# Three pairs of k tiles instead of two in two products, and a multiplication moved to ScalarE

## The chip, the cores and the metric

The kernel runs on one core of a Trainium2 chip. The metric is the time of one execution on the device in microseconds (us). Three runs of the kernel before took 1409.82, 1412.84 and 1413.8 us; the median is 1412.84 us.

## The reference

One block of a streaming encoder on 256 tokens of width 2048, in float32. Cut to what matters here:

```python
z = rms_norm(x, norm_mix_w) @ w_in                    # 2048 -> 11264
# an HGRN2 recurrence gives y_a, chunked attention gives y_b
merged = gate_a * (y_a @ w_branch_a) + gate_b * (y_b @ w_branch_b)
h = x + merged @ w_out                                # 2048 -> 2048
u = rms_norm(h, norm_mlp_w)
h = h + square(relu(u @ w_up)) @ w_down               # 2048 -> 8192 -> 2048
out = rms_norm(h, norm_final_w)
```

The change lies between `merged @ w_out` and `u @ w_up`.

## The kernel before, in words

**Precision.** Every float32 operand is split into a high part of a rounded type (fp32r) and a low part, the rest. A product of two tiles is three matmuls, high by high, high by low and low by high (`mm3`, L143 to L145). The split (`split`, L88) is a cast on ScalarE (L89) and a subtraction on VectorE (L90). Weights come from HBM in pieces of 128 x 1024 (two k tiles of 512 columns), are split in the same way, and lie in eight raw and six high and six low buffers.

**The GEMM unit.** Most of the gates, w_out, w_up and w_down go through `gemm_s` (L718). A unit makes 256 tokens by 1024 output columns, as a 2 x 2 arrangement of accumulators: two blocks of 128 tokens (`m`) by two blocks of 512 columns (`n`). The 16 k tiles of 128 would give 16 x 4 = 64 products. For some k tiles it uses the scheme of Strassen and Winograd: k tile k is paired with k tile k + 4, and each pair takes seven products (named p1 to p7) in place of eight, at the price of additions of weight pieces on VectorE (`add`, L742) and of sums of activation blocks that are made once (`combos`, `S2`, `S4`, `S5`, `S7`, which have three pairs each). The parameter `r` says how many pairs go through the scheme. With `r=2` the weights of the scheme are four whole pieces (`W11`, `W12`, `W21`, `W22`). With `r=3` the third pair's weights come in two more pieces, `X` and `Y`, that each hold two halves from different places, with additions of 512 columns, three more whole splits (`px`, `py`, `px2`) and a half one (`p4y`). The k tiles left over are plain products (`plain`): with `r=2` six pairs of k tiles for each `n`, with `r=3` five, the first of which is k tiles 3 and 7.

**The order in a unit.** p1, p3, p5, p2; then `flush()` does what the unit before left for later (its last plain product and the end of its second column block); then p6, a plain product, p7. If the second remaining pair of k tiles needs only activation blocks that exist (`early`, L843), another plain product comes next, then p4. Otherwise half of a plain product stands ahead of p4 and half behind it. Then `between()` is called, which turns activations for what follows; the remaining plain products end the unit. In the `early` order the first plain products behind `between()` are on the first two pairs of k tiles in the list of those left over; in the other order on the second alone, which is k tiles 8 and 9 with `r=3`.

**The three units around the change.** `wo0` and `wo2` are the two units of w_out, `up00` and `up02` the first two of w_up. At `between()` of `wo2` stands `h_blocks(0)`, at that of `up00` `h_blocks(2)` (L932). For two blocks n and two token blocks m each, it transposes h with four PE transposes into one PSUM bank (two banks are there for this), multiplies by the norm's weight, which is one factor per partition for each group of 128 columns, into `tmp` (`hw`, L941), splits that into the high and low part of `hT` (ScalarE and VectorE), and sums the squares of h on ScalarE (`hsq`, L943). `h_blocks(0)` then makes the sums S from `hT`. At the start of `up00` two of the four blocks of `hT` exist; the first w_down unit `dn00` starts in the same way with two blocks of its own activations.

**What sets the order of the work.** A planner orders the instructions of each engine by priority, mostly program order, with its own estimate of when inputs and buffers are ready; work marked with high priority (weight splits, additions of pieces, evictions) goes ahead on its engine. Each engine then takes its instructions in that order. All weights are loaded through SP's queue; ScalarE and POOL issue a few other transfers.

Of the kernel before, what the change touches and what calls it, by code (L numbers as in the profile page):

```python
# [11 lines left out]
AF = mybir.ActivationFunctionType  # L12
ALU = mybir.AluOpType
# [3 lines left out]
P = 128  # L17
# [4 lines left out]
FF = 8192  # L22
NC = 512
# [13 lines left out]
def bc(ap, pos, n):  # L37

    dims = [list(d) for d in ap.ap]
    dims.insert(pos, [0, n])  # L40
    return bass.AP(tensor=ap.tensor, offset=ap.offset, ap=dims)
# [9 lines left out]
def tile_hybrid_block(  # L51
# [5 lines left out]
    nc = tc.nc  # L57
# [13 lines left out]
    wmix, wmlp = vt[:, 0:16], vt[:, 16:32]  # L71
# [16 lines left out]
    def split(hi, lo, src, copy=None):  # L88
        (copy or nc.scalar.copy)(hi, src)  # L89
        nc.vector.tensor_tensor(lo, src, hi.bitcast(F32), op=ALU.subtract)  # L90
# [7 lines left out]
    def new_act(what):  # L98

        return apool.tile([P, 4, 2, T], F32R, name=f"act_{what}", tag="act")  # L100

    def transpose4(src, what):

        tp = turns_in.tile([P, 4, P], F32, name=f"tp_{what}", tag="tp")
        for j in range(4):
            nc.tensor.transpose(tp[:, j, :], src[:, j * P:(j + 1) * P], ident)
        return tp
# [42 lines left out]
    def gemm(lhs, w, n0, nkt, what, wide=False, between=None):  # L150

        acc = new_acc(what)
        for kt, wh, wl in weights(w, n0, nkt, NC, what, wide=wide):
            if between and between[0][0] == kt:
                between.pop(0)[1]()
            for m in range(NM):
                mm3(acc[:, m, :], *lhs_of(lhs, kt, m), wh, wl, kt == 0, kt == nkt - 1)
        return acc
# [48 lines left out]
    done = [0, 0]  # L207
    for kt, n in zip(starts, steps):
        c, a = kt // 4, kt % 4
# [376 lines left out]
    for g in range(2):  # L586
        qT = [qk_chunk(C_AQ + g * NC + i * T, f"aq{g}{i}", rstd8_t, None if g or i else acc_q0) for i in range(2)]
        kT = [qk_chunk(C_AK + g * NC + i * T, f"ak{g}{i}", rstd_t) for i in range(2)]
        acc = gemm(xT, w_in_n, C_AV + g * NC, KD, f"av{g}")
# [14 lines left out]
    def token(what):  # L604
        return tk.tile([P, NC], F32, name=what, tag="t", bufs=TOK)
# [7 lines left out]
    R = 3  # L613
# [36 lines left out]
    for n in range(2):  # L650
        acc = gemm(xT, w_in_t, C_GA + n * NC, KD, f"ga{n}", wide=True)
# [52 lines left out]
    def gemm2(lhs, w, n0, nkt, what):  # L704

        acc = [bank(f"{what}{m}") for m in range(NM)]
        for k in range(0, nkt, 2):
            wh, wl = parts(piece(w, f"{what}{k}", (n0, k), (n0, k + 1)), f"{what}{k}")
            for m in range(NM):
                for a in range(2):  # L710
                    mm3(acc[m], *lhs_of(lhs, k + a, m), wh[:, a], wl[:, a], k + a == 0, k + a == nkt - 1)
        return acc

    def evict(dst, acc):
        with tc.high_priority(offset=2000):
            nc.vector.tensor_tensor(dst, acc, dst, op=ALU.add)
# [178 lines left out]
    for gates, c, col, what, fresh in ((ga, 2, C_GA, "ga", True), (gb, 0, C_GB, "gb", True), (gb, 2, C_GB, "gb", False)):  # L895
        gates += [[None] * NM for _ in range(2)]

        def done(m, n, acc, gates=gates, c=c, what=what):
            gates[c + n][m] = sigmoid(token(f"gate_{what}{c + n}{m}"), acc, m)
# [5 lines left out]
    mT = []  # L905
# [8 lines left out]
    for n in range(4):  # L914
        for y, w, gate, what in ((ya, w_branch_a, ga[n], "ba"), (yb, w_branch_b, gb[n], "bb")):
            acc = gemm2(y, w, n * NC, 8, f"{what}{n}")
            for m in range(NM):
                nc.vector.tensor_tensor(gate[m], acc[m], gate[m], op=ALU.mult)
            if what == "ba" and n:
                turn(n - 1)  # L920
                if n == 2:
                    Sm = combos(mT, "m", "b")
# [4 lines left out]
    h1 = [[None] * NM for _ in range(4)]  # L927
    ssq2 = small.tile([P, NM, 4], F32, name="ssq2", tag="ssq2")
    hT = []
    Sh = {}  # L930

    def h_blocks(n0):  # L932

        for n in (n0, n0 + 1):
            hT.append(new_act(f"h{n}"))
            hi, lo = hT[n][:, :, 0, :], hT[n][:, :, 1, :]
            for m in range(NM):
                t = h1[n][m]
                tp = transpose4(t, f"h{n}{m}")
                tmp = tk.tile([P, 4, P], F32, name=f"hw_{n}_{m}", tag="t", bufs=TOK)  # L940
                nc.vector.tensor_tensor(tmp, tp, bc(wmlp[:, 4 * n:4 * n + 4], 2, P), op=ALU.mult)  # L941
                split(hi[:, :, m * P:(m + 1) * P], lo[:, :, m * P:(m + 1) * P], tmp)
                nc.scalar.activation(token(f"hsq_{n}_{m}"), t, AF.Square, accum_out=ssq2[:, m, n:n + 1])  # L943
        if not n0:
            Sh.update(combos(hT, "h", "a"))
            return
        ssum2 = small.tile([P, NM], F32, name="ssum2", tag="ssum")
        nc.vector.tensor_reduce(ssum2, ssq2, axis=AX.X, op=ALU.add)
        rsqrt(rstd2, ssum2, D, NM)

    rstd2 = const.tile([P, NM], F32, name="rstd2")
    for n0 in (0, 2):
        for n in (n0, n0 + 1):
            for m in range(NM):
                t = token(f"h1_{n}_{m}")
                nc.gpsimd.dma_start(t, x[m * P:(m + 1) * P, n * NC:(n + 1) * NC])
                h1[n][m] = t
        gemm_s(mT, Sm, w_out, n0 * NC, f"wo{n0}", lambda m, n, acc, n0=n0: evict(h1[n0 + n][m], acc), r=2 if n0 else R,
               between=lambda: h_blocks(0) if n0 else turn(3))


# [3 lines left out]
    NQ = 4  # L965
    for qd in range(NQ):
        last = qd == NQ - 1
        uT = []
        pend = []

        def turn():

            c, rs = pend.pop(0)
            uT.append(new_act(f"u{qd}{c}"))
            hi, lo = uT[-1][:, :, 0, :], uT[-1][:, :, 1, :]
            for m in range(NM):
                tp = transpose4(rs[m], f"u{qd}{c}{m}")
                if c < 2:
                    blocks[m, c] = tk.tile([P, pairs, P], F32, name=f"a{m}{c}_u{qd}", tag="t", bufs=TOK)
                    nc.scalar.copy(blocks[m, c], tp[:, :pairs])  # L980
                split(hi[:, :, m * P:(m + 1) * P], lo[:, :, m * P:(m + 1) * P], tp)

        Su = {}
        blocks = {}
        pairs = R if last else 4

        def turns():
            if len(hT) == 2:
                h_blocks(2)
            while pend:  # L990
                turn()
            if len(uT) == 2:
                Su.update(combos(uT, f"u{qd}", "b", [blocks[m, j] for m in range(NM) for j in range(2)], pairs))

        for c in range(0, 4, 2):
            rs = {}

            def done(m, n, acc, c=c, rs=rs):
                t = token(f"r{qd}{c}")
                with tc.high_priority(offset=2000):  # L1000
                    nc.scalar.activation(t, acc, AF.Relu, scale=rstd2[:, m:m + 1])
                nc.scalar.activation(t, t, AF.Square)
                rs[m, n] = t
                if m == NM - 1:
                    pend.append((c + n, [rs[i, n] for i in range(NM)]))

            gemm_s(hT, Sh, w_up, qd * (FF // NQ) + c * NC, f"up{qd}{c}", done, r=R if qd or c else 2, between=turns)
        if last:
            wf = apool.tile([P, D], F32, name="wf", tag="act")
            nc.gpsimd.dma_start(wf, bass.AP(tensor=norm_final_w.tensor, offset=norm_final_w.offset, ap=[[0, P], [1, D]]))  # L1010

        def out_of(m, n, acc, last=last):
            r = h1[n][m]
            if n > 1 and not last:
                t = token(f"y{qd}{n}{m}")
                with tc.high_priority(offset=2000):
                    nc.scalar.copy(t, acc)
                nc.gpsimd.dma_start(r, t, accum_op=ALU.add)
                return
            evict(r, acc)  # L1020
            if not last:
                return
            nc.scalar.activation(token(f"ysq_{n}_{m}"), r, AF.Square, accum_out=ssq3[:, m, n:n + 1])
            if n < 3:
                nc.vector.tensor_tensor(r, r, wf[:, n * NC:(n + 1) * NC], op=ALU.mult)
                return
            nc.vector.tensor_reduce(ssum3[:, m:m + 1], ssq3[:, m, :], axis=AX.X, op=ALU.add)
            rsqrt(rstd3[:, m:m + 1], ssum3[:, m:m + 1], D, 1)
            f = rstd3[:, m:m + 1]
            for i in range(4):  # L1030
                t = h1[i][m]
                if i == 3:
                    nc.vector.scalar_tensor_tensor(t, t, f, wf[:, i * NC:(i + 1) * NC], op0=ALU.mult, op1=ALU.mult)
                elif i == 2:
                    nc.vector.tensor_scalar(t, t, f, None, op0=ALU.mult)
                else:
                    nc.scalar.activation(t, t, AF.Copy, scale=f)
                (nc.sync if i % 2 else nc.scalar).dma_start(out[m * P:(m + 1) * P, i * NC:(i + 1) * NC], t)

        for n0 in (0, 2):  # L1040
            gemm_s(uT, Su, w_down, n0 * NC, f"dn{qd}{n0}", lambda m, n, acc, n0=n0: out_of(m, n0 + n, acc), r=pairs if n0 else R, kt0=qd * KD,
                   between=None if n0 else turns, tail=last and n0 == 2)
# [44 lines left out]
```

## Time and profile before

| | |
|---|---|
| median of three runs | 1412.84 us (1409.82 to 1413.8) |
| the profiled execution | 1409.94 us |
| its span, from the first to the last instruction | 1408.2 us |
| mean granted TensorE clock | 0.998 |
| busy: PE, VectorE, ScalarE | 1395.7, 1143.0, 875.5 us |

PE is TensorE's matmul, PEld its weight load, DVE VectorE, ACT ScalarE, POOL GpSimd, SP the queue that issues most transfers. `L143` is line 143. A group's row gives its line, engine, operation, `out<-in` by the program's names (without buffer numbers), how many there were, and the shortest, median and longest in ns with the first and last start in us; or the busy time in us and the mean in ns of one, and behind a second bar the idle time of the engine in front of them with what ended it. A row of the timeline begins with start and duration in us. A row of stretches has, for each engine, busy time and number of instructions. Matmuls overlap, so the time that one costs is read from the starts of neighbours.

### The profile page before, as it was taken

How to read it: one execution, taken by the hardware profiler on the slowest of the kernel's cores; microseconds unless marked ns; L12 is line 12 of the kernel's file. 1: busy time of each engine (PE TensorE's matmuls, PEld its weight loads, DVE VectorE, ACT ScalarE, POOL GpSimd, SP SyncE). 2: the span in 40 equal slices, each digit the busy share in tenths (PEclk: the TensorE clock that was granted, in tenths of full speed). 3: DMA queues.
4: the chain of work that ended last, by engine and by line, in shares of the span. 5: the costliest groups of instructions: out<-in, count | busy, mean ns of one | idle time of the engine just before them, and what ended most of it. 6: DMA issues, size and time to landing. Idle time of an engine off the chain costs nothing.

```text
span 1408.2 us, 18448 instructions
## 1 busy us (share of the span) xinstructions
PE 1395.7 (99%) x6620; PEld 1160.2 (82%) x6620; DVE 1143.0 (81%) x1493; ACT 875.5 (62%) x1176; POOL 44.5 (3%) x104
## 2 busy tenths in 40 slices
PE   9999999999999999999999999999999999999997
PEld 8889888878788888888888888888888888888886
DVE  7898987575768784688998979889798898979984
ACT  6767745464655664446666766668556875658753
POOL 3000001010000000000000000000000000000000
PEclk9999999999999999999999999999999999999999
DMA  9654545555456766646654565755568554687542
GB/s 334 220 180 144 178 143 167 189 165 179 155 178 210 239 202 215 211 164 225 224 193 143 174 224 194 246 208 157 196 225 268 195 176 154 224 269 239 175 158 102
DMA packets 122157, 275.97 MB, mean 196 GB/s; under 512 B 10193, under 2 KB 31441, under 8 KB 121681
## 3 DMA queue, kind: packets, MB, share of 16 engines
q1 hardware_dynamic: 117600, 264.80, 55.8%
q0 software_dynamic: 3312, 8.39, 2.6%
q10 hardware_dynamic: 1152, 1.60, 0.3%
q8 instruction: 52, 0.85, 0.2%
q14 instruction: 41, 0.33, 0.1%
HBM read 269.51 MB, written 2.10 MB: 193 GB/s over the span
## 4 chain that ended last, share of the span: by engine, by line
PE 95%; DVE 2%; issue 1%; ACT 1%; DMA 1%; POOL 0%; POOLq 0%; ACTq 0%; DVEq 0%
PE acc_ak L175 2%; PE acc_aq L175 2%; PE acc_hf L175 2%; PE acc_hq L175 1%; PE ps L393 1%; PE acc_ga L144 1%; PE acc_hg L145 1%; PE acc_hg L143 1%; PE acc_bb L143 1%; PE acc_ga L145 1%; PE acc_ga L143 1%; PE acc_hg L144 1%; PE acc_av L143 1%; PE acc_ba L145 1%; PE acc_ba L144 1%; PE acc_ba L143 1%
## 5 line engine op out<-in xcount | busy, mean ns | idle before, releaser
L742 DVE TENSOR_TENSOR raw_dn<-raw_dn,raw_dn 128x1024 f32<-128x1024 f32 x44 | 53.2, 1215 | 0.0
L175 PE MATMUL acc_aq<-act_x,wh_aq 128*128 128x512 f32 x128 | 46.4, 401 | 0.0
L175 PE MATMUL acc_hq<-act_x,wh_hq 128*128 128x512 f32 x128 | 45.8, 396 | 0.0
L175 PE MATMUL acc_hf<-act_x,wh_hf 128*128 128x512 f32 x128 | 45.8, 395 | 0.0
L175 PE MATMUL acc_ak<-act_x,wh_ak 128*128 128x512 f32 x128 | 45.0, 397 | 0.0
L742 DVE TENSOR_TENSOR raw_up<-raw_up,raw_up 128x1024 f32<-128x1024 f32 x32 | 39.1, 1221 | 0.5
L174 PE MATMUL acc_aq<-act_x,wl_aq 128*128 128x256 f32 x120 | 34.6, 288 | 0.0
L90 DVE TENSOR_TENSOR wl_av<-raw_av,wh_av 128x1024 fp32r<-128x1024 f32 x16 | 19.6, 1223 | 18.1 <-ACT wh_av L89 18.1
L174 PE MATMUL acc_hf<-act_x,wl_hf 128*128 128x256 f32 x120 | 34.1, 284 | 0.0
L174 PE MATMUL acc_hq<-act_x,wl_hq 128*128 128x256 f32 x120 | 34.0, 283 | 0.0
L174 PE MATMUL acc_ak<-act_x,wl_ak 128*128 128x256 f32 x120 | 33.6, 280 | 0.0
L90 DVE TENSOR_TENSOR wl_ba<-raw_ba,wh_ba 128x1024 fp32r<-128x1024 f32 x16 | 19.6, 1224 | 16.6 <-ACT wh_ba L89 16.6
L89 ACT CAST wh_ba<-raw_ba 128x1024 fp32r<-128x1024 f32 x16 | 16.9, 1053 | 24.3 <-PE acc_ba L145 10.0
L90 DVE TENSOR_TENSOR wl_bb<-raw_bb,wh_bb 128x1024 fp32r<-128x1024 f32 x16 | 19.6, 1222 | 14.7 <-ACT wh_bb L89 14.7
L90 DVE TENSOR_TENSOR wl_aq<-raw_aq,wh_aq 128x1024 fp32r<-128x1024 f32 x16 | 19.6, 1224 | 14.4 <-ACT wh_aq L89 14.2
L89 ACT CAST wh_bb<-raw_bb 128x1024 fp32r<-128x1024 f32 x16 | 16.9, 1054 | 22.8 <-PE acc_ba L145 12.8
L90 DVE TENSOR_TENSOR wl_ga<-raw_ga,wh_ga 128x1024 fp32r<-128x1024 f32 x16 | 19.6, 1224 | 13.8 <-ACT wh_ga L89 13.8
L89 ACT CAST wh_aq<-raw_aq 128x1024 fp32r<-128x1024 f32 x16 | 16.8, 1047 | 22.2 <-PE acc_hg L145 10.9
L89 ACT CAST wh_av<-raw_av 128x1024 fp32r<-128x1024 f32 x16 | 16.8, 1052 | 22.0 <-PE acc_av L145 12.4
L89 ACT CAST wh_hg<-raw_hg 128x1024 fp32r<-128x1024 f32 x16 | 16.7, 1044 | 20.7 <-PE acc_hg L145 9.7
L175 PEld LDWEIGHTS acc_aq<-act_x,wh_aq 128*128 128x128 f32 x128 | 24.1, 188 | 5.5 <-issue 0.7
L175 PEld LDWEIGHTS acc_ak<-act_x,wh_ak 128*128 128x128 f32 x128 | 23.9, 188 | 5.5
(1551 smaller groups left out, 5128.9 us busy)
## 6 DMA issues: line engine op xcount, KB each, us to landing
raw_dn<-in_w_down_dram SPq DMA_DIRECT2D x44, 512.0 KB, 5.6
raw_up<-in_w_up_dram SPq DMA_DIRECT2D x32, 512.0 KB, 7.6
raw_ga<-in_w_in_t_dram SPq DMA_DIRECT2D x20, 512.0 KB, 4.4
raw_hi<-in_w_in_n_dram SPq DMA_DIRECT2D x16, 512.0 KB, 4.0
raw_hg<-in_w_in_n_dram SPq DMA_DIRECT2D x16, 512.0 KB, 3.5
raw_aq<-in_w_in_t_dram SPq DMA_DIRECT2D x16, 512.0 KB, 3.9
raw_ak<-in_w_in_t_dram SPq DMA_DIRECT2D x16, 512.0 KB, 3.6
raw_av<-in_w_in_n_dram SPq DMA_DIRECT2D x16, 512.0 KB, 4.1
```

Source lines behind the costliest of these rows:

```text
L89: (copy or nc.scalar.copy)(hi, src)
L90: nc.vector.tensor_tensor(lo, src, hi.bitcast(F32), op=ALU.subtract)
L143: nc.tensor.matmul(acc, hi, wh, start=first, stop=False, skip_group_check=True)
L144: nc.tensor.matmul(acc, hi, wl, start=False, stop=False, skip_group_check=True)
L145: nc.tensor.matmul(acc, lo, wh, start=False, stop=last, skip_group_check=True)
L174: nc.tensor.matmul(acc[:, cb, 0:T], wl[:, c], r[:, 0, :], start=False, stop=False)
L175: nc.tensor.matmul(acc[:, cb, :], wh[:, c], r.rearrange("p u t -> p (u t)"), start=kt == 0, stop=kt == nkt - 1)
L393: nc.tensor.matmul(ps[:, m, :], klf[:, a * P:(a + 1) * P], qrf[:, a * 192:(a + 1) * 192], start=True, stop=True)
L742: nc.vector.tensor_tensor(dst, dst, t, op=ALU.add)
```

## The change

Two things. The units `wo2` and `up00` use three pairs of k tiles, as every other unit already does but for the second w_down units of the first three quarters, which use four. And in `h_blocks` the multiplication of a transposed block (128 x 4 x 128, in PSUM) by the norm's weight is no longer one VectorE instruction of 512 columns but four ScalarE instructions of 128 columns, each with one factor per partition. It concerns eight blocks, four in `wo2` and four in `up00`.

```diff
@@ h_blocks
                 tp = transpose4(t, f"h{n}{m}")
                 tmp = tk.tile([P, 4, P], F32, name=f"hw_{n}_{m}", tag="t", bufs=TOK)
-                nc.vector.tensor_tensor(tmp, tp, bc(wmlp[:, 4 * n:4 * n + 4], 2, P), op=ALU.mult)
+                for j in range(4):
+                    nc.scalar.activation(tmp[:, j], tp[:, j], AF.Copy, scale=wmlp[:, 4 * n + j:4 * n + j + 1])
                 split(hi[:, :, m * P:(m + 1) * P], lo[:, :, m * P:(m + 1) * P], tmp)
@@ the units of w_out
-        gemm_s(mT, Sm, w_out, n0 * NC, f"wo{n0}", lambda m, n, acc, n0=n0: evict(h1[n0 + n][m], acc), r=2 if n0 else R,
+        gemm_s(mT, Sm, w_out, n0 * NC, f"wo{n0}", lambda m, n, acc, n0=n0: evict(h1[n0 + n][m], acc),
                between=lambda: h_blocks(0) if n0 else turn(3))
@@ the units of w_up
-            gemm_s(hT, Sh, w_up, qd * (FF // NQ) + c * NC, f"up{qd}{c}", done, r=R if qd or c else 2, between=turns)
+            gemm_s(hT, Sh, w_up, qd * (FF // NQ) + c * NC, f"up{qd}{c}", done, between=turns)
```

`R` is 3 and the default of `r`, so leaving `r` out makes it 3.

## The prediction

> **What bounds the kernel now.** I read the page first: the shares of the engines, the granted clock and the chain that ended last.
>
> ```profile
> span 1408.2 us, 18448 instructions
> PE 1395.7 (99%) x6620; PEld 1160.2 (82%) x6620; DVE 1143.0 (81%) x1493; ACT 875.5 (62%) x1176; POOL 44.5 (3%) x104
> ...
> PEclk9999999999999999999999999999999999999999
> ...
> PE 95%; DVE 2%; issue 1%; ACT 1%; DMA 1%; POOL 0%; POOLq 0%; ACTq 0%; DVEq 0%
> ```
>
> PE is busy from end to end at full clock, and 95% of the chain is PE. A busy PE could still be a stretched one, so next I looked at the starts of neighbouring matmuls, in order of time.
>
> ```profile
> 716.41 0.39 PE L143 MATMUL acc_wo2c<-wh_wo2r,act_m 128*128 128x512 f32 x1
> ...
> 718.46 0.39 PE L143 MATMUL acc_wo2c<-wh_wo2r,act_m 128*128 128x512 f32 x1
> ...
> 720.04 0.39 PE L143 MATMUL acc_up00c<-wh_up00p,S_h 128*128 128x512 f32 x1
> ```
>
> Nine steps lie between the first two rows: (718.46 - 716.41) / 9 = 0.228 us a matmul. A record lasts 0.39 us because neighbours overlap; 0.228 us is the price. To the third row there are seven more steps, (720.04 - 718.46) / 7 = 0.226 us, across the change from one GEMM's products to the next's: no gap. So PE's stream is the bound, and only two things move the end: matmuls added or dropped, and a PE made to wait. Next, the stretches from each GEMM's first matmul to the next one's (w_out second unit, w_up first unit, w_up second unit):
>
> ```profile
> core 0: us, PE busy (x) PEld busy (x) DVE busy (x) ACT busy (x) POOL busy (x), PEclk, DMA share, GB/s
> ...
> 673.00:717.10 44.10, 44.10 (x204) 36.34 (x203) 41.04 (x50) 27.86 (x39) 0.00 (x0) 1.00 0.54 184
> 717.10:761.20 44.10, 44.10 (x203) 36.37 (x202) 37.04 (x42) 28.90 (x39) 1.68 (x1) 1.00 0.57 189
> 761.20:804.70 43.50, 43.50 (x201) 36.07 (x200) 39.11 (x46) 34.12 (x49) 0.00 (x0) 1.00 0.57 194
> ```
>
> The first two have two pairs now; the third already has three, turns activations in the same place, and PE never stands still in it. VectorE's 41.04 of 44.10 us in the first is the number to watch.
>
> **Matmuls.** These are the products of the second w_out unit on one of its three lines:
>
> ```profile
> L143 PE MATMUL acc_wo2c<-wh_wo2r,act_m x48: 388/389/481, 682.5 to 724.6; 128*128 128x512 f32 x48
> ...
> L143 PE MATMUL acc_wo2c<-wh_wo2p,S_m x8: 389/389/389, 674.6 to 685.9; 128*128 128x512 f32 x8
> ...
> L143 PE MATMUL acc_wo2c<-wh_wo2p,act_m x6: 389/389/389, 673.0 to 690.0; 128*128 128x512 f32 x6
> ```
>
> 48 plain and 14 of the seven-product scheme make 62. A pair of k tiles costs 8 plain products or 7 in the scheme, so with three pairs it is 40 + 21 = 61. Each product is three matmuls: 3 fewer in each of the two GEMMs, 6 in all, 6 x 0.228 = **-1.37 us**. All of it is on the path. The sums S of activations are already made for three pairs, so they cost nothing more.
>
> **VectorE, ScalarE and the queue.** Prices, from the three-pair unit that exists and from ScalarE instructions of like shape:
>
> ```profile
> L742 DVE TENSOR_TENSOR raw_up02y<-raw_up02y,raw_up02x x2: 691/692/692, 753.7 to 762.3; 128x512 f32<-128x512 f32 x2
> L90 DVE TENSOR_TENSOR wl_up02px<-raw_up02x,wh_up02px x2: 1218/1221/1224, 751.7 to 767.5; 128x1024 fp32r<-128x1024 f32 x2
> L941 DVE TENSOR_TENSOR hw<-tp_h,vt x8: 678/684/691, 691.7 to 739.6; 128x512 f32<-128x512 f32 x8
> L89 ACT CAST wh_wo2r<-raw_wo2r 128x1024 fp32r<-128x1024 f32 x12 | 12.6, 1053 | 6.5 <-PE acc_wo2c L145 4.3 <-issue 1.4 <-ACT hsq L943 0.7
> L683 SPq DMA_DIRECT2D raw_up02x<-in_w_up_dram x2: 368/415/462, 733.7 to 734.1; - x2
> L464 ACT ACTIVATE osq<-po 128x128 f32<-128x128 f32 x16 | 4.3, 271 | 0.1
> L562 ACT ACTIVATE sb<-sb,mx 128x128 f32<-128x128 f32 x16 | 6.4, 401 | 1.5 <-DVE mx L559 1.5
> L481 ACT ACTIVATE act_ya<-tpo,hgw x8: 458/471/487, 151.1 to 231.1; 128x256 fp32r<-128x256 f32 x8
> L1001 ACT ACTIVATE r<-acc_up00c,rstd x4: 688/690/690, 754.7 to 772.8; 128x512 f32<-128x512 f32 x4
> L89 ACT CAST act_h<-hw x8: 614/617/620, 692.4 to 741.2; 128x512 fp32r<-128x512 f32 x8
> 740.12 1.66 ACT L89 CAST act_h<-hw 128x512 fp32r<-128x512 f32 x3
> ```
>
> For each GEMM, three pairs add four half-width additions on VectorE (4 x 0.692 = 2.77 us) and change the splits: 7 + 12 = 19 whole ones become 7 + px + py + px2 + half a p4y + 10 = 20.5, so 1.5 more (VectorE 1.83 us, ScalarE 1.5 x 1.053 = 1.58 us). The bytes loaded stay the same, but X, Y and the two loads of k tiles 3 and 7 take two transfers each: 4 more issues, about 4 x 0.415 = 1.7 us of SP's queue, on which only other weight loads stand behind. None of this is on the path while pieces arrive ahead of PE, so I cost it at nothing; the cover is counted below.
>
> The moved multiplication: VectorE loses 8 x 0.684 = 5.5 us. ScalarE gains 32 instructions of 128 columns. The trace has none with both a PSUM source and a factor per partition at that width; 256 columns take 0.471 and 512 take 0.690, a slope of 0.86 ns a column, so 0.36 us. The nearest rows bound it: 0.271 (PSUM source, no factor) and 0.401 (a per-partition operand, with accumulation). In a row they overlap: three casts of 0.617 take 1.66 us, 0.095 less for each start. A block of four takes 4 x 0.36 - 3 x 0.095 = 1.16 us (0.80 to 1.32) against 0.684 on VectorE. In each of the two stretches ScalarE gains 4 x 1.16 + 1.58 = 6.2 us: 27.9 and 28.9 us become 34.1 and 35.1 of 43.4, so there is room.
>
> VectorE's load in the first stretch becomes 41.04 + 2.77 + 1.83 - 2.74 = 42.9 of 43.4 us: full, which by itself is no wait, since pieces lie ready ahead. How far ahead is seen behind the transposes of h, where VectorE is tightest:
>
> ```profile
> 714.23 2.35 DVE L90 TENSOR_TENSOR wl_up00p<-raw_up,wh_up00p 128x1024 fp32r<-128x1024 f32 x2
> ```
>
> The first of these two ends at 714.23 + 1.22 = 715.4 and is the piece that PE takes up at 720.04 in the row above (the scheme's third product, p5): a lead of 4.6 us. After the change PE's stretch from the transposes to there loses 24 plain matmuls, which now come earlier (5.5 us), and gains two times three (1.4 us): 4.1 us shorter. VectorE's work there loses four multiplications (2.74) and two splits (2.44) and gains a split (1.22) and two half additions (1.38): 2.6 us less. The lead falls to 4.6 - 4.1 + 2.6 = 3.1 us. Still ahead: no wait. The ends are 0 and all that VectorE gains, 2 x (2.77 + 1.83 - 2.74) = 3.7 us; I take 0, since the lead is left.
>
> **The transposes' release.** Only two banks hold transposes, so block three waits for the multiplication of block one, and PE's queue stands in order behind it.
>
> ```profile
> 690.65 1.04 PE L106 MATMUL tp_h<-ident,h 128*128 128x128 f32 x8
> ...
> 692.22 0.39 PE L143 MATMUL acc_wo2c<-wh_wo2r,act_m 128*128 128x512 f32 x1
> 692.46 0.66 PE L106 MATMUL tp_h<-ident,h 128*128 128x128 f32 x4
> 692.87 0.47 PE L144 MATMUL acc_wo2c<-wl_wo2r,act_m 128*128 128x512 f32 x1
> ...
>   DVE hw L941: 1.1, 4
> ```
>
> The four waits that the trace lists are of weight loads, 0.27 us each. On PE they cost nearly nothing: 692.22 to 692.87 is 0.65 us for a matmul (0.228) and four transposes (0.41). The planner puts the third block where the first is multiplied, to within 0.1 us, and fills the time with plain matmuls. With ScalarE the release is 1.16 - 0.68 = 0.5 us later, and a weight cast of 1.05 us may stand in front. Four blocks wait so: bounds 0 (planned later again) and 4 x 1.53 = 6.1 us. I take 0.3 us, near the lower end, since the rows show the planner's times to fit.
>
> The Trainium skill ("ScalarE: Activation LUTs", Rules for kernel authors) gives multiplications to VectorE and not to ScalarE, and in "What ACT_TABLE_LOAD costs" it prices an instruction with one pointer operand at 0.28 us plus 0.833 ns an element: 0.386 us here, an estimate from that page. By it a block would take 4 x 0.386 - 3 x 0.093 = 1.27 us. This trace agrees within its bounds; whether the rule decides the time depends on the release above, which is the second rival.
>
> **The order in the first w_up unit.** With two pairs, two plain products' worth on k tiles 6 and 7 come ahead of the transposes of h, and 24 matmuls that need no new h stand behind them. With three pairs the condition on k tile 9 fails and the other branch is taken: behind the transposes stands at once a product on k tiles 8 and 9, which need the new h. Uncovered, PE would wait from its transposes (0.87 us for two blocks) to the last of transpose, multiplication and cast, 0.66 + 1.16 + 0.62 = 2.4 us: 1.6 us, and some 0.4 us for a second block. The first w_down unit has that branch already:
>
> ```profile
> 806.59 0.60 PE L106 MATMUL tp_u<-ident,r 128*128 128x128 f32 x4
> 806.95 0.48 PE L143 MATMUL acc_dn00c<-wh_dn00p,S_u 128*128 128x512 f32 x1
> ...
> 827.47 1.03 PE L106 MATMUL tp_u<-ident,r 128*128 128x128 f32 x8
> 828.26 0.48 PE L143 MATMUL acc_dn00c<-wh_dn00r,act_u 128*128 128x512 f32 x1
> ```
>
> There the planner took one block 21 us early, behind the first products, and the plain products follow the other two without a gap. Bounds 0 and 2.0 us; I take 0.2 us, since the same branch costs nothing there.
>
> **Sum:** -1.37 + 0.3 + 0.2 = -0.9 us. The profiled execution took 1409.94 us (span 1408.2) and would come to 1409.0. It lies 2.9 us under the median of the runs, 1412.84; against that median I say **1411.9 us**.
>
> **Rivals.**
> - First, the uncovered order: no block is taken early, and the w_up unit waits its 2.0 us. Net -1.37 + 0.3 + 2.0 = +0.9: 1413.8 us. For it: the two-pair unit takes no block early. Against it: the three-pair unit in the rows above does.
> - Second, ending on the other side: ScalarE's release. All four later blocks wait 1.53 us: net -1.37 + 6.1 = +4.8, 1417.6 us. It decides for slower once the four waits together pass 1.37 us, and for slower by over 0.3% (4.2 us) from 5.6 us. For it: every block is 0.5 us dearer, and weight casts go ahead of it by priority. Against it: the twelve casts of that unit's plain pieces (row above) have 6.5 us of idle time in front of them, most of it waiting for PE to free a buffer.
> - Third, VectorE becomes the bound where it is 42.9 of 43.4 us full: the 3.1 us of lead go to pieces that the planner puts in front, and all that VectorE gains lies on the path. Net -1.37 + 3.7 + 0.5 (the two terms of the sum) = +2.8, 1415.7 us. For it: the load. Against it: the third stretch, with like work, runs at 39.11 of 43.50 us and no wait.
>
> **From these to the numbers.** The sum 0.60, first rival 0.14, second 0.16, third 0.10. 0.3% of 1412.84 is 4.2 us, about what a measurement of this kernel can tell from no change (its three runs lie 4.0 us apart). The sum's case and the first lie within it but for the scatter of medians (0.04 faster, 0.04 slower); of the second some 0.11 lies above it, of the third half: slower 0.20, same 0.76. The low end, 1408.4, is the sum with all waits at nothing, 1411.5, less the 3 us by which single runs lie under the median; the high end, 1417.8, takes in all three rivals.
>
> **What would show it.** Right: 61 products in both GEMMs; their stretches at 43.4 us or a little more; 128-column multiplications of 0.27 to 0.40 us; a block of h transposed early in the w_up unit. Wrong: gaps of over 0.5 us on PE behind the third and fourth block (second rival), in front of k tile 8 of the w_up unit (first), or a matmul of p5 or p2 waiting for VectorE's low part (third). The prediction fails if the planner, given other costs, reorders much that comes later.

## The result, and the profile after

Six runs of the changed kernel have a median of 1424.13 us (1422.43 to 1425.81), six of the kernel before beside them 1411.18 us (1409.45 to 1413.8). The ratio is 1.0093, with a 95% interval of 1.0083 to 1.0103: 13 us slower, where 0.9 us less was forecast and the range ended at 1417.8. The profiled execution's span is 1421.8 us against 1408.2.

From the page of the kernel after, the head, the clock and the chain:

```profile
span 1421.8 us, 18484 instructions
PE 1398.9 (98%) x6614; PEld 1161.2 (82%) x6614; DVE 1147.1 (81%) x1497; ACT 887.0 (62%) x1212; POOL 43.3 (3%) x104
...
PE 93%; DVE 3%; ACT 2%; issue 1%; DMA 0%; POOL 0%; SPq 0%; POOLq 0%; ACTq 0%; DVEq 0%
```

Six matmuls fewer, as forecast, but more of the chain now lies on VectorE and ScalarE (3% and 2%, before 2% and 1%). PE's waits between 600 and 800 us (what waited, for what; total us, times, longest), and the stretches that hold them:

```profile
PE acc_up00c L143 <- ACT S_h L89: 6.3, 1, 6.3
PE tp_h L106 <- ACT hw L942: 3.1, 2, 2.7
PE acc_up00c L143 <- ACT act_h L89: 1.2, 1, 1.2
```

```profile
673.20:719.60 46.40, 43.73 (x201) 35.77 (x200) 37.52 (x41) 32.20 (x54) 0.00 (x0) 1.00 0.55 182
717.00:734.00 17.00, 10.76 (x51) 8.44 (x49) 16.70 (x22) 8.28 (x10) 0.00 (x0) 0.97 0.37 123
734.00:740.00 6.00, 5.90 (x14) 4.40 (x15) 2.38 (x4) 2.32 (x4) 0.00 (x0) 0.51 0.01 2
```

The first of these is the second w_out unit (44.10 us before). VectorE was forecast full there, 42.9 us; it is busy for 37.52 of 46.40 us and finishes 41 instructions where it had 50. It has time left over and PE waits all the same; the work that it did not do there falls into the second stretch, where it is busy for 16.70 of 17.00 us. The last shows PE at a granted clock of 0.51. In order of time on PE:

```profile
697.73 0.40 PE L145 MATMUL acc_wo2c<-wh_wo2r,act_m 128*128 128x512 f32 x1
700.80 0.66 PE L106 MATMUL tp_h<-ident,h 128*128 128x128 f32 x4 [2.67 <-ACT hw L942]
...
721.64 0.60 PE L106 MATMUL tp_h<-ident,h 128*128 128x128 f32 x4
...
727.28 0.49 PE L106 MATMUL tp_h<-ident,h 128*128 128x128 f32 x3
734.10 0.80 PE L143 MATMUL acc_up00c<-wh_up00p,S_h 128*128 128x512 f32 x1 [6.33 <-ACT S_h L89]
...
739.05 0.63 PE L143 MATMUL acc_up00c<-wh_up00p,S_h 128*128 128x512 f32 x1
739.48 0.59 PE L144 MATMUL acc_up00c<-wl_up00p,S_h 128*128 128x512 f32 x1
...
752.74 0.60 PE L106 MATMUL tp_h<-ident,h 128*128 128x128 f32 x4
754.56 0.50 PE L143 MATMUL acc_up00c<-wh_up00r,act_h 128*128 128x512 f32 x1 [1.22 <-ACT act_h L89]
755.36 0.39 PE L144 MATMUL acc_up00c<-wl_up00r,act_h 128*128 128x512 f32 x1
756.21 0.66 PE L106 MATMUL tp_h<-ident,h 128*128 128x128 f32 x4 [0.46 <-ACT hw L942]
```

From the starts of neighbours, less the usual pitch of 0.227 us for a matmul and 0.11 us for a transpose: the third transposed block costs 700.80 - 697.73 - 0.23 = 2.8 us; the first product on the sums S of h 734.10 - 727.28 - 3 x 0.11 = 6.5 us; behind it 13 matmuls run 0.43 us apart in place of 0.227 (739.48 - 739.05 = 0.43), with the steps in between 2.85 us in all; two waits behind `between()` of the w_up unit, one for the cast of a new block in front of k tile 8 and one for a transpose bank, cost (754.56 - 752.74 - 0.44) + (756.21 - 755.36 - 0.23) = 1.4 + 0.6 = 2.0 us. With the matmuls saved: 2.8 + 6.5 + 2.85 + 2.0 - 1.4 = 12.8 of the span's 13.6 us; the other 0.8 us is not placed.

Why the block and the sums are late is read on the other engines. SP's loads of the plain pieces, then ScalarE, then VectorE (start, duration; in brackets the idle time before and what ended it):

```profile
659.43 0.80 SPq L683 DMA_DIRECT2D raw_wo2r<-in_w_out_dram  x2
674.25 3.73 SPq L680 DMA_DIRECT2D raw_wo2r<-in_w_out_dram  x2
679.93 0.80 SPq L683 DMA_DIRECT2D raw_wo2r<-in_w_out_dram  x2
682.20 7.68 SPq L680 DMA_DIRECT2D raw_wo2r<-in_w_out_dram  x6
```

```profile
692.05 0.63 ACT L942 ACTIVATE hw<-tp_h,vt 128x128 f32<-128x128 f32 x2
695.39 2.95 ACT L89 CAST wh_wo2r<-raw_wo2r 128x1024 fp32r<-128x1024 f32 x3 [2.71 <-DMA raw_wo2r<-in_w_out_dram]
698.24 0.36 ACT L942 ACTIVATE hw<-tp_h,vt 128x128 f32<-128x128 f32 x1
698.50 1.98 ACT L89 CAST wh_wo2r<-raw_wo2r 128x1024 fp32r<-128x1024 f32 x2
700.38 0.36 ACT L942 ACTIVATE hw<-tp_h,vt 128x128 f32<-128x128 f32 x1
```

```profile
696.47 1.23 DVE L90 TENSOR_TENSOR wl_wo2r<-raw_wo2r,wh_wo2r 128x1024 fp32r<-128x1024 f32 x1 [4.59 <-ACT wh_wo2r L89]
...
711.14 0.55 DVE L624 TENSOR_TENSOR a_h<-act_h 128x384 f32<-128x384 f32 x1
...
712.21 0.68 DVE L90 TENSOR_TENSOR act_h<-hw,act_h 128x512 fp32r<-128x512 f32 x1
712.81 1.22 DVE L90 TENSOR_TENSOR wl_up00p<-raw_up,wh_up00p 128x1024 fp32r<-128x1024 f32 x1
...
729.82 1.49 DVE L624 TENSOR_TENSOR a_h<-act_h 128x384 f32<-128x384 f32 x3
```

For comparison the kernel before: its early loads, VectorE's last low parts of h and the end of the sums, and PE's first product on them:

```profile
654.89 4.62 SPq L680 DMA_DIRECT2D raw_wo2r<-in_w_out_dram  x3
...
670.62 15.68 SPq L680 DMA_DIRECT2D raw_wo2r<-in_w_out_dram  x9
...
697.26 1.89 DVE L90 TENSOR_TENSOR act_h<-hw,act_h 128x512 fp32r<-128x512 f32 x3
...
700.67 1.49 DVE L624 TENSOR_TENSOR a_h<-act_h 128x384 f32<-128x384 f32 x3
...
710.29 0.55 DVE L90 TENSOR_TENSOR S_h<-a_h,S_h 128x384 fp32r<-128x384 f32 x1
...
718.68 0.39 PE L143 MATMUL acc_up00c<-wh_up00p,S_h 128*128 128x512 f32 x1
```

Before, three plain pieces of w_out are issued before 660 us and nine from 670.6 us on; after, one (two transfers of half a piece) and the rest from 674.25 us on. A cast then waits 2.71 us for its transfer; behind it stand, in ScalarE's order, the third and fourth multiplication of the first block, which frees the PSUM bank that the third block's transposes need (700.38 + 0.36 = 700.74, and they start at 700.80). VectorE stands idle for 4.59 us. Then the work on h is late: the last block's low part is made at 712.21 (before, all were made by 699.2), and three of the sums' first four additions, ready to go then, stand behind 17 us of weight pieces of w_up and evictions, until 729.82. Before, the sums ended at 710.29 + 0.55 = 710.84 us, 7.8 us ahead of the first product on them at 718.68 us. That lead stood in no step of the prediction.

### The profile page after: what moved, and what is told of

The parts are those of the page before. It is cut to its first block, busy times and chain, and to the rows that moved or that the text cites. A ratio compares the mean times of both kernels' runs of the same rounds, so it can differ in the third digit from the quotient of the medians.

```text
span 1421.8 us, 18484 instructions
## 1 busy us (share of the span) xinstructions
PE 1398.9 (98%) x6614; PEld 1161.2 (82%) x6614; DVE 1147.1 (81%) x1497; ACT 887.0 (62%) x1212; POOL 43.3 (3%) x104
## 4 chain that ended last, share of the span: by engine, by line
PE 93%; DVE 3%; ACT 2%; issue 1%; DMA 0%; POOL 0%; SPq 0%; POOLq 0%; ACTq 0%; DVEq 0%
PE acc_ak L175 2%; PE acc_aq L175 2%; PE acc_hf L175 2%; PE acc_hq L175 1%; PE ps L393 1%; PE acc_ga L144 1%; PE acc_hg L143 1%; PE acc_hg L145 1%; PE acc_ga L145 1%; PE acc_bb L143 1%; PE acc_bb L145 1%; PE acc_ga L143 1%; PE acc_hg L144 1%; PE acc_ba L145 1%; PE acc_av L145 1%; PE acc_ba L143 1%
## 5 line engine op out<-in xcount | busy, mean ns | idle before, releaser
L175 PEld LDWEIGHTS acc_hf<-act_x,wh_hf 128*128 128x128 f32 x128 | 24.0, 188 | 5.5 <-DVE f L183 0.3
```

The source lines that it names most:

```text
L175: nc.tensor.matmul(acc[:, cb, :], wh[:, c], r.rearrange("p u t -> p (u t)"), start=kt == 0, stop=kt == nkt - 1)
```

## The experiments

The theories. **A**: the multiplication on ScalarE makes the blocks late. **G**: the two scheme pieces more (X and Y) hold raw buffers, so the plain weights come late. **H**: the order; two plain products less stand behind the transposes as cover. **D**: VectorE's order; the sums of h stand behind pieces of high priority. **F**: VectorE simply has too much to do. Other letters in the quoted expectations say there what they stand for. Each median below stands against runs of the kernel before made beside it (medians of 1410.36 to 1410.68 us).

### The parts one at a time

`act_only`: the kernel before with the multiplication moved, two pairs everywhere.

```diff
-                nc.vector.tensor_tensor(tmp, tp, bc(wmlp[:, 4 * n:4 * n + 4], 2, P), op=ALU.mult)
+                for j in range(4):
+                    nc.scalar.activation(tmp[:, j], tp[:, j], AF.Copy, scale=wmlp[:, 4 * n + j:4 * n + j + 1])
```

> The multiplication on ScalarE alone, two pairs in both units as before. Theory A (ScalarE's multiplications, in turn with the weight casts, make h late by themselves): several us of PE waiting in front of the first product on the sums of h, +5 us or more. Rival B (three pairs in the second w_out unit make weights and sums late, whoever multiplies): no wait there, within 1.5 us of the kernel before. Rival C (only the two together): as B, +0 to +2 us.

Measured 1411.08 us, ratio 1.0002 (0.9993 to 1.0012), no wait of PE in these units. The move alone costs nothing: A falls as a cause by itself. It does use up the lead: the sums end at 727.3 us in place of 710.8, but the first product on them then stands at 723.0 us, behind other products, and PE does not wait. So a lost lead alone is not yet a loss.

`three_only`: the kernel after with the multiplication back on VectorE (the diff above, reversed).

> Three pairs in both units, the multiplication left on VectorE. A: 6 matmuls fewer and the uncovered order's wait in the first w_up unit, -1.4 + 2.0, so within 1 us of the kernel before. B: PE waits 6 us or more in front of the first product on the sums of h, +8 us or more. C: as A, at most +3 us.

Measured 1420.78 us, 1.0073 (1.0058 to 1.0088): waits of 2.0 us at the third block and 5.9 us at the sums, and half clock behind the second. With the third pairs alone most of the loss is there, 10.3 of 13.0 us; the rest comes with the move on top of them, and the two intervals overlap a little.

`three_wo2_act`, `three_up00_act` and `three_wo2_dve`: three pairs in one of the two units, the other back at two; in the third also the multiplication on VectorE.

```diff
@@ the units of w_out (three_up00_act, from the kernel after)
-        gemm_s(mT, Sm, w_out, n0 * NC, f"wo{n0}", lambda ...: evict(...),
+        gemm_s(mT, Sm, w_out, n0 * NC, f"wo{n0}", lambda ...: evict(...), r=2 if n0 else R,
@@ the units of w_up (three_wo2_act and three_wo2_dve)
-            gemm_s(hT, Sh, w_up, qd * (FF // NQ) + c * NC, f"up{qd}{c}", done, between=turns)
+            gemm_s(hT, Sh, w_up, qd * (FF // NQ) + c * NC, f"up{qd}{c}", done, r=R if qd or c else 2, between=turns)
```

> Three pairs in the second w_out unit alone, with the multiplication on ScalarE. All theories: the wait in front of the sums' first product stays; without the uncovered order of the first w_up unit it is some 2 us less than the changed kernel, about +10 to +11 us. If it is under +5 us, the first w_up unit's own three pairs (its X and Y additions on VectorE ahead of the sums) are part of the cause.

> Three pairs in the first w_up unit alone, with the multiplication on ScalarE. A: the wait in front of the sums' first product stays, +7 us or more. B: no such wait; the 2.0 us of the uncovered order less 0.7 us of matmuls, about +1 us. C: between the two, if the X and Y additions of the w_up unit go ahead of the sums on VectorE, +3 us or more.

> Three pairs in the second w_out unit alone, the multiplication left on VectorE. Theory G (the w_out unit's plain weights land late because its six scheme pieces hold the raw buffers; casts and splits then bunch up and hold the blocks of h): nearly as slow as the same with ScalarE's multiplication (1421.4 us), 1418 to 1422 us, the third block waiting 2 us for VectorE. If the multiplication's engine matters here, under 1415 us.

Measured 1421.38 us (1.0077, 1.006 to 1.0093), 1414.8 us (1.0035, 1.0022 to 1.0048) and 1420.39 us (1.0064, 1.0048 to 1.0081). The w_out unit alone costs 9.7 us with the multiplication on VectorE; the move adds about 1 us to it, within the two intervals. The w_up unit alone, with the move, costs some 4 us, 3 us more than B expected; four waits add up to 3.1 us of it, and the rest is not placed. PE's waits of `three_wo2_dve`, then the two longest of `three_up00_act`:

```profile
PE acc_up00c L143 <- ACT S_h L89: 4.7, 1, 4.7
PE tp_h L106 <- DVE hw L941: 2.5, 1, 2.5
```

```profile
PE tp_h L106 <- ACT hw L942: 1.4, 1, 1.4
PE acc_up00c L143 <- ACT wh_up00p L89: 0.7, 1, 0.7
...
```

So the question is narrow: why does the third pair in the w_out unit, without any change to the multiplication, make the third block wait 2.5 us and the sums nearly 5?

### Priorities (theory D)

The kernel after with the work on h moved up in the planner's order: the sums alone, the multiplication and split alone, or all of it, in both units.

```diff
+                with tc.high_priority(offset=2000):     # prio_blocks, prio_all: multiplication and split
+            with tc.high_priority(offset=2000):         # prio_sums, prio_all
                 Sh.update(combos(hT, "h", "a"))
```

> The changed kernel with the making of the sums S of h at the high priority that weight splits have. Theory D (the sums are late because the planner lets the first w_up unit's splits and piece additions go ahead of them on VectorE): the wait of 6.3 us in front of the sums' first product shrinks by most of itself and the half-clock matmuls with it, some 5 to 9 us off the changed kernel; but the last block of h itself still has normal priority, so it may shrink little. Theory F (VectorE has more work there than fits): the wait only moves to the pieces behind, total within 2 us of the changed kernel.

> Only the multiplication and the split of the blocks of h at high priority, the sums not. Theory E (late blocks are the cause: plain weights of the w_out unit arrive late, their casts and splits bunch up and hold the blocks): the third block's wait of 2.8 us goes and the sums follow, 8 us or more off the changed kernel. D: the blocks come earlier, but the sums still stand behind the w_up pieces; at most 5 us off.

> As the run with the sums at high priority, and the multiplication and the split of the blocks of h too. D: the wait in front of the sums' first product is gone; with it go 6.5 + 2.7 us, so +3 to +5 us against the kernel before stay (the third block's wait and the uncovered order of the first w_up unit). F: PE waits instead for the pieces of p5, p2 or p6, total still +8 us or more.

Measured 1423.32 us (1.0091), 1425.69 us (1.0112) and 1417.79 us (1.0055, 1.004 to 1.007). Each half alone leaves the wait for the sums at 6.2 to 6.3 us. In `prio_sums` the low part of the last block, which the sums need and which has ordinary priority, is left behind the pieces and made at 732.09 us. In `prio_blocks` it is made at 710.83 us, but three of the sums' first additions still stand until 729.41 us. Both together take that wait and the half clock away. The third block's wait stays at 1.8 us, and waits of 0.2 to 0.9 us come up in the w_up units, so that against the kernel before 7.4 us of 13.0 are left, between what D and F expected. D is a part of the cause, and F could still be the other.

### The order (theory H)

`sooner` is the kernel after with the transposes of h one product earlier in the w_out unit; `later` is the kernel before with them 24 matmuls later, so that as few stand behind them as with three pairs.

```diff
@@ sooner, from the kernel after
         adds(W21, W11)
         early = left[1][1] // 4 < len(lhs)
+        if between and sooner:
+            between()
...
-        if between:
+        if between and not sooner:
             between()
@@ later, from the kernel before
-        if between:
+        if between and what != "wo2":
             between()
...
         plains(0, *left[0 if early else 1:2])
+        if between and what == "wo2":
+            between()
         plains(1, *left[2 if early else 1:2])
```

In both only the w_out unit's `between()` is moved (`sooner` is true there alone).

> The changed kernel with the turning of h in the second w_out unit placed one plain product and p4 earlier (some 21 matmuls, 4.8 us of PE). If the lost cover is the cause (84 matmuls between the turning and the next unit in place of 108), 5 us or more of the wait go and the half clock too: 7 to 9 us off. If the blocks are held by late weights (E) they are as late as before: within 2 us of the changed kernel.

> The kernel before with two pairs everywhere; in the second w_out unit the transposes of h stand 24 matmuls later in the program, behind the plain products on the first two pairs of the first column block, so that 84 matmuls are left behind them as with three pairs, and not 108. Theory H: the sums of h come up to 5.5 us later, past the products that need them: a PE wait of 3 to 6 us in front of the first w_up unit's p3 and a half clock behind it, 1414 to 1419 us. Theory G: the lead that the sums have in the kernel before takes it, no wait of over 0.7 us, 1410 to 1412.

Measured 1423.93 us (1.0097), with nearly the waits of the kernel after, and 1411.79 us (1.0008, 0.9998 to 1.0017) with one wait of 0.8 us. In `sooner` the third block does come some 3.4 us earlier in its unit, and the wait for the sums is still 6.3 us. A cover of 84 matmuls in place of 108 does no harm by itself, and an earlier place in the program does not help: H falls as a cause by itself.

### The buffers (theory G)

`wo2_dve_more_raw`, `more_raw` and `prio_all_more_raw` give the plain pieces of the w_out unit two buffers of their own, free at that time, on top of `three_wo2_dve`, the kernel after and `prio_all`.

```diff
-        raw = buf("raw", F32, what)
+        if what[:5] in ('wo2r0', 'wo2r1'):
+            raw = apool.tile([P, 2 * NC], F32, name=f"raw_{what}", tag="act")
+        else:
+            raw = buf("raw", F32, what)
```

> As that, with the plain weight pieces of the second w_out unit in two buffers of the activations' pool that are free then, so that they needn't wait for the eight raw buffers; everything is computed. G: the loads start some 10 us earlier, no cast waits for a transfer, the third block's wait goes and the sums are in time: within 2 us of the kernel before. If the lost cover or VectorE's load decides (F): at most 3 us off the run without them.

> The changed kernel with the same two more buffers for the second w_out unit's plain pieces. G: the third block's wait (2.8 us), the sums' wait (6.5) and the half clock (2.7) go; 2.0 us of the w_up unit's uncovered order less 1.4 us of matmuls stay: +1 to +3 us against the kernel before. F: +9 us or more.

> Both remedies: high priority for the blocks and the sums of h, and the two more buffers. If late loads are what was left of the run with priority (+7.4 us): +1 to +3 us. If what was left is the w_up unit's pieces that now yield on VectorE: +5 us or more.

Measured 1419.48 us (1.0062), 1424.91 us (1.0101) and 1423.52 us (1.0089). The times are those that F and the late w_up pieces were expected to give, but the waits are others, so they told nothing of G or F: the planner loaded pieces of w_up into the eight buffers that this left free, and the plain pieces of w_out, now in few buffers, came later than before (waits of 3.0, 5.7 and 5.7 us for their high parts). The wait for the sums was gone in all three and the time was not: it had moved.

`hold` and `hold_later` go the other way round: two pairs everywhere, but two raw buffers taken in the w_out unit where X and Y would be, without and with the order of `later`.

```diff
+        def hold():
+            if what == "wo2":
+                t = buf("raw", F32, f"{what}hold{len(held_raw)}")
+                nc.sync.dma_start(t[:, 0:1], w[n0 // NC, 0, :, 0, len(held_raw):len(held_raw) + 1])
+                held_raw.append(t)
+        def let_go():
+            if held_raw:
+                nc.vector.tensor_copy(small.tile([P, 1], F32, ..., tag="go"), held_raw.pop(0)[:, 0:1])
...
```

> The kernel before with two pairs everywhere; in the second w_out unit two raw weight buffers are taken where X and Y would stand (one column of 512 bytes in all is loaded into each) and given back where X and Y end, one behind p6 and one behind p4. Nothing else is added, so matmuls, splits and additions are those of before. Theory G (raw buffers held, so plain weights come late): the third transposed block of h waits 1 us or more, the sums of h come late, 1415 to 1420 us. Theory H (order and cover): no PE wait of over 0.5 us, within 1.5 us of the kernel before, 1410 to 1412. If VectorE's added work is the cause and neither of the two: no change either.

> Both edits together, held buffers and transposes 24 matmuls later, still with two pairs everywhere. If the two together are the cause and the third pair's arithmetic on VectorE is not: near the unit with three pairs alone and no multiplication moved, less its three matmuls that it doesn't save, 1418 to 1422 us, with the wait for the sums and the half clock. If the third pair's additions and splits on VectorE are needed for it: no more than the dearer of the two runs above plus 1 us, and below 1416.

Measured 1434.76 us (1.0167) and 1436.02 us (1.0176), neither of them for the reason under test. The stretch from 420 to 460 us, long ahead of the edit, in `hold` and in `hold_long` below:

```profile
420.00:460.00 40.00, 40.00 (x174) 32.28 (x173) 31.77 (x32) 23.74 (x29) 0.00 (x0) 1.00 0.60 198
```

```profile
420.00:460.00 40.00, 40.00 (x178) 33.14 (x177) 32.69 (x33) 25.05 (x29) 0.00 (x0) 1.00 0.60 203
```

Nothing tied the two copies to the products, and they gave the buffers back at 667 us, before the unit began (682.5 us there, 673.0 us in the kernel before); `hold` has no wait of PE. But the matmuls of the GEMMs run 2% slower, 174 in place of 178 in 40 us, with the granted clock at 1.00: over some 5500 matmuls of 512 columns 4 to 5 ns each make the 24 us. What was expected under either theory missed, and the runs say nothing on G.

`hold_long` mends this: the release adds a column of p7's copied result, so it can't go ahead of p7, and no new tile is made.

```diff
+        def let_go(u):
+            for t in held_raw:
+                nc.vector.tensor_tensor(t[:, 0:1], t[:, 0:1], u[:, 0:1], op=ALU.add)
...
+        let_go(u2)
```

> The kernel before with two pairs everywhere; in the second w_out unit two raw weight buffers are taken where X and Y would stand (one column is loaded into each) and given back only when p7's result has been copied out (VectorE adds one column of that copy to each), as late as X and Y are given back with three pairs. No other work is added. Theory G (held buffers make the plain weights late and bunch their splits): loads of the plain pieces about 3 us later, a wait of 1 us or more at the third transposed block or at the sums of h, 1413 to 1420 us. If the third pair's splits and additions are needed for the loss: at most small waits, 1410 to 1412.

Measured 1412.53 us, 1.002 (1.0011 to 1.003). PE's only wait here, VectorE's release and the sums' end:

```profile
PE tp_h L106 <- DVE hw L956: 0.9, 1, 0.9
```

```profile
687.65 0.23 DVE L743 TENSOR_TENSOR raw_wo2hold<-raw_wo2hold,u_wo 128x1 f32<-128x1 f32 x2 [2.57 <-ACT u_wo L786]
...
725.61 1.02 DVE L90 TENSOR_TENSOR S_h<-a_h,S_h 128x384 fp32r<-128x384 f32 x2
```

One plain piece is loaded early, as after, not three; the third block waits; the sums end at 726.6 in place of 710.8 us, with no lead left over, but PE is not held up by them. The release itself makes VectorE wait 2.57 us, so not all of this is the buffers'. The time lies between the two expectations. G by itself costs 2 us at most; it uses up the lead, and something has to come on top for the loss. That this is the third pair's own work is argued and not shown: the held buffers together with the later order, without that work, stand in no run that answers, since `hold_later` did not.

### Late transfers and the sums' place together

`half_bytes` is `three_wo2_dve` with plain pieces of w_out that load only their first k tile, used for both: half of the bytes of ten loads, and the products on the second k tiles with their own weights, are left out; buffers, casts, splits and matmuls are the same.

```diff
+        if what[:5] in ("wo2r0", "wo2r1"):
+            nc.sync.dma_start(raw[:, :NC], w[n0 // NC, k0 // kpr, :, k0 % kpr, :])
+            return raw, "half"
...
```

`half_bytes_prio` adds `prio_all`'s priorities in the w_out unit alone.

> Three pairs in the second w_out unit alone, the multiplication left on VectorE, as in the run that took 1420.4; but each plain weight piece of that unit loads only its first k tile, which is used for both of its k tiles: half of the bytes of ten loads, about 2.6 MB, are left out, and the products on the second k tiles are with other weights. Buffers, casts, splits and matmuls stay the same. Theory G in the form that the transfers take long once they start late: they land sooner, the third block's wait and the sums' wait shrink by more than half, 1411 to 1416. If the buffers' release sets the time whatever the bytes, or VectorE's order does: waits of 2 and 5 us as before, 1418 to 1422.

> Three pairs in the second w_out unit alone, multiplication on VectorE, plain pieces of that unit with half of their bytes (their second k tile's weights are left out and the first's used again), and the multiplication, split and sums of the first four blocks of h at the priority of the weights. If late transfers and the sums' place on VectorE are the two causes: no PE wait of over 0.7 us, no stretch at half clock, 1409.5 to 1412 us, three matmuls (0.7 us) under the kernel before. If VectorE has simply too much to do there: the waits come back elsewhere, 1413 to 1416, near the 1415.7 of the run without the priority.

Measured 1415.65 us (1.0034, 1.0021 to 1.0047) and 1410.05 us (0.9996, 0.9987 to 1.0006). PE's waits of the first, and the w_out unit of the second:

```profile
PE acc_up00c L143 <- ACT S_h L89: 3.5, 1, 3.5
PE tp_h L106 <- DVE hw L947: 0.3, 1, 0.3
```

```profile
675.10:718.60 43.50, 43.50 (x201) 35.90 (x200) 41.87 (x52) 28.74 (x41) 0.00 (x0) 1.00 0.41 139
```

With half of the bytes the third block's wait goes from 2.5 to 0.3 us and 4.7 of the 9.7 us are gone; the wait for the sums, 4.7 us, falls to 3.5 and not by half as expected. The last five loads of plain pieces are issued at the same place in the unit, but they land a median of 3.5 us later in place of 6.5 us: fewer bytes change when a piece arrives, not when its load starts. With the priorities as well there is no wait of PE and no half clock, the unit takes 43.5 us, where 43.4 were forecast for it, and VectorE does 41.87 us of work in it. So F falls for this unit: the work fits. What stopped it was that operands came late and that the sums stood in the wrong place; mended together, these two make up the whole 9.7 us there. What the priorities alone would do in this unit was not measured, so the 9.7 us are not divided between the two. The some 4 us that the w_up unit costs were not taken apart like this.

## Why the prediction was wrong, by its own steps

- **Matmuls, -1.37 us.** Right: 6614 in place of 6620, and the w_out unit holds 201 starts where it held 204.
- **VectorE, ScalarE and the queue, at nothing.** This is the step that failed. The bytes stay the same, but two whole pieces more sit in the eight raw buffers until the scheme has done with them, so one plain piece and not three comes early. The cover was counted from one lead, that of p5's low part (4.6 to 3.1 us), and from busy time per unit; the sums, made by the same engine at ordinary priority, had 7.8 us and were not looked at. A bound of 3.7 us on VectorE's added work was no bound on what its order could cost: 6.5 us, and behind it 2.85 us of half clock, for which the prediction had no term. In the w_out unit alone late operands and the place of the sums, mended together, give all 9.7 us back.
- **ScalarE's price, 0.36 us each and 1.16 us a block.** Right, as the row of the 32 and a block that runs undivided show:

```profile
L942 ACT ACTIVATE hw<-tp_h,vt x32: 344/372/423, 692.1 to 761.2; 128x128 f32<-128x128 f32 x32
...
701.77 1.14 ACT L942 ACTIVATE hw<-tp_h,vt 128x128 f32<-128x128 f32 x4
```

  The Trainium skill's price ("ScalarE: Activation LUTs", "What ACT_TABLE_LOAD costs"), an estimate of 0.386 us each and 1.27 us a block, is near too. The Trainium skill's rule to multiply on VectorE ("ScalarE: Activation LUTs", Rules for kernel authors) did not decide anything: `act_only` is 1.0002.
- **The transposes' release, +0.3 us.** 2.8 us at the third block of the w_out unit and 0.6 us in the w_up unit. The bound allowed one cast between multiplications; five stood there, and the first of them waited for its transfer. The ground for staying near the lower end, that the planner's times fit to 0.1 us, did not hold: here the block stands 2.7 us too early. `three_wo2_dve` has the wait at 2.5 us with the multiplication on VectorE, so the cause is not the move.
- **The order in the w_up unit, +0.2 us.** The planner did transpose two blocks early, at 721.64 us and by 727.28 us, but ScalarE multiplies the first of them only at 749.99 us and casts it at 753.89 us, behind three weight casts (751.00 + 2.99), and the product on k tile 8 waits 1.4 us for that cast. An early transpose is no cover if the rest of the block is left for later. With the 0.6 us of the release the waits come to 2.0 us; that this is the upper bound and the first rival's price is luck, for that rival had no block taken early.
- **The rivals.** The third named the right engine (VectorE's pieces put in front behind the transposes) but a wrong reason, a full engine, and so a price of 3.7 us. The second was right that weight casts can stand in front of a block on ScalarE, but had it at all four later blocks and with one cast each; `act_only` shows that ScalarE's own work alone brings no wait.
- **What would show it wrong.** Two of the three signs came, the gap at the third block and the one in front of k tile 8. The third sign was p5 or p2 waiting for a low part. It was the products on the sums, waiting for a high part: the first, at 734.10 us, is p6's, on S2, whose cast ends then, and p3 follows at 735.12 us with the cast of S4.

## What to carry to other kernels

Busy time that fits is not cover: for each result that PE will ask for, the sums as well as the weights, take its lead from the trace, and see what stands in front of it on its engine if its inputs come later. Where a change puts more pieces into a fixed set of buffers, look at when each load was issued before, and how many were early, not only at bytes. Work at ordinary priority behind a stream of high-priority pieces was the first to starve here; the blocks and the sums at high priority together with weights in time gave the 9.7 us back.

## What the runs showed of the hardware

After a wait PE can run at half its rate: behind the 6.3 us wait 13 matmuls 0.43 us apart, behind the 3.5 us wait of `half_bytes` some eight. The Trainium skill ("TensorE: Matmul & The Clock Gate", Part 1) puts a throttle to half clock behind one idle window of about 3.4 us, on a window that runs freely. These two waits agree with it. Waits shorter than that show no one rule here: behind 2.45 us in `three_wo2_dve` seven matmuls are at half rate (granted clock 0.59 from 705.4 to 708 us), behind 2.16 us in `sooner` the clock is 0.50 from 699 to 702 us,

```profile
705.43 0.76 PE L106 MATMUL tp_h<-ident,h 128*128 128x128 f32 x4 [2.45 <-DVE hw L941]
705.85 0.77 PE L144 MATMUL acc_wo2c<-wl_wo2r,act_m 128*128 128x512 f32 x1
706.42 0.63 PE L145 MATMUL acc_wo2c<-wh_wo2r,act_m 128*128 128x512 f32 x1
```

while behind the 2.67 us of the kernel after (700.80) none is. So here a wait of some 2.2 to 2.7 us may or may not cost some 1.5 us more, and one of 3.5 us or more brought half clock in each run that had one.

In `hold` and `hold_later` every matmul of 512 columns is 5 ns longer from start to start (a median of 0.232 for 0.227 us) at full granted clock, far ahead of the edit too. They differ from `hold_long`, where it is 0.227 us, by the release (two copies at 666 and 667 us in place of two additions) and by the tile that the copies write, four bytes a partition in the pool of small tiles (four buffers). A guess is that the tile moved what is laid out behind it in SBUF. That was not tried by itself, so the cause stays open; when a kernel is slower everywhere, the pitch of its matmuls is worth a look.
